# The reciprocal square roots of a hybrid trunk's norms, moved from VectorE to a power operation on GpSimd

## The chip, the cores and the metric

The kernel runs on one core of one Trainium2 chip. The metric is the time of one execution in device microseconds (us), lower is better.

## The reference

One layer of a decoder trunk on 2048 rows of width 1024. The input is normed and projected; four head groups work on the projection; each is normed per head (three of them) and gated, and an output projection with a norm of its own is added to the input:

```python
def _rmsnorm(x, g):
    y = x32 * lax.rsqrt(jnp.mean(x32 * x32, axis=-1, keepdims=True) + EPS)
    return (y * g.astype(F32)).astype(x.dtype)
def _head_rmsnorm(o, g):
    return o * lax.rsqrt(jnp.mean(o * o, axis=-1, keepdims=True) + EPS) * g.astype(F32)
def _l2norm(t):
    return t * lax.rsqrt(jnp.sum(t * t, axis=-1, keepdims=True) + EPS)
...
h = _rmsnorm(x, norm_pre[i])
p = jnp.einsum('bld,dc->blc', h, w_in[i]).astype(F32)
y_ret  = retention(...)        # chunks of 64, then _head_rmsnorm and silu(gate)
y_dn   = gated delta rule(...) # q, k through _l2norm; a recurrence over chunks of 64; _head_rmsnorm, gate
y_s5   = diagonal state space, gelu, a gate
y_gla  = gated linear attention(...)  # chunks of 16, a recurrence; _head_rmsnorm, gate
o = jnp.einsum('bld,md->...', concatenate([y_ret, y_dn, y_s5, y_gla]), w_out[i])
x = x + _rmsnorm(o, norm_post[i])
```

## The kernel before

The 2048 rows are 16 tiles of 128. The program runs in stages, by the trace at these times: to 140 us the input norms (`p0_x`, one call a tile) with the weights' scaling, projections and the first retention tiles; to 330 us the rest of retention (`ret_rest`, a tile a call); 330 to 612 us GLA (`phase_gla`, 16 iterations, two tiles' scores in flight, with S5 work put between); 612 to 1060 us DeltaNet (`phase_dn`, eight steps of two tiles: `dn_pre` makes decays and the norms of q and k, `dn_back` runs the recurrence over the state VS); from 1060 us the output (`phase_out`, whose `back` makes one tile and whose fronts load and transpose later ones, two ahead).

Wherever a norm needs 1/sqrt(v), `rsqrt` (L171) makes it with nine VectorE instructions on a [128, n] tile, n being 1, 4 or 8: a first guess from the bits of v (L175, L176), then two rounds of polynomial steps (L181 to L187), each needing the one before. It is called from four places, 88 calls in all:

- `p0_x`, 16 times (n = 1, tile names x..): ScalarE squares and sums (L484), VectorE scales and adds eps (v, L486), rsqrt, and ScalarE makes h (L491).
- `finish` (L345), 48 times (n = 4, names f..), for retention, GLA and DeltaNet, 16 each: ScalarE squares the branch's output o from PSUM into fsq (L349), VectorE sums it per head (fss, L351), scales and adds eps (fv, L354 or, with DeltaNet's eps per head, L356), rsqrt gives fry, L359 multiplies by half the gate's scale (frr), and four multiplications (L363) make o times frr times gate, which goes to memory.
- `dn_pre`, 8 times (n = 8, names d..): rk = rsqrt(kk), sk = kk rk (L1450), and rk squared (L1451), which scales dD and dkgd, and by them the mask dmb (L1459).
- `back`, 16 times (n = 1, names o..): VectorE squares and sums the output of (ojk, L1721), sums the four parts (ost, L1724), makes e2 and ov (L1726, L1728), rsqrt, and xo = ot times r plus xo (L1733), while GpSimd makes ot = of times the gain (L1722).

Each engine executes its instructions in the order in which the scheduler put them. The scheduler takes the program's streams (generators that yield between pieces) and interleaves them by priority; the instructions of a norm so come to stand between those of other tiles. In DeltaNet the recurrence goes through VectorE's VS = dQ - c (L1669) and ScalarE's copy of the next state; in GLA through gS (L1237, VectorE) and gSbd (L1240, GpSimd). GpSimd also does the masks and products of the scores (gE, L1160 to L1176), the S5 powers (s5c, s5O; L608), DeltaNet's dKG (L1659, L1660), the head of the convolution (raw, L1336) and a part of the weights' scaling (w, L243).

Of the kernel before, what the change touches and what calls it, by code (L numbers as in the profile page):

```python
# [16 lines left out]
EPS = 1e-6  # L17
XS = 6
BLK = 1040
MAGIC = float(0x5F1FFFF9)  # L20
# [125 lines left out]
class Trunk:  # L146
# [24 lines left out]
    def rsqrt(self, pool, v, n, tag, mul=1.0):  # L171

        nc = self.nc
        yi = self.t(pool, [128, n], tag + "y", I32)
        nc.vector.tensor_scalar(yi, v.bitcast(I32), 1, None, op0=ALU.arith_shift_right)  # L175
        nc.vector.tensor_scalar(yi, yi, -1.0, MAGIC, op0=ALU.mult, op1=ALU.add)  # L176
        y = yi.bitcast(F32)
        t = self.t(pool, [128, n], tag + "t")
        V = nc.vector
        m = 0.375 * mul  # L180
        V.tensor_tensor(t, y, y, op=ALU.mult)  # L181
        V.scalar_tensor_tensor(t, t, -0.703952253 * m, v, op0=ALU.mult, op1=ALU.mult)
        V.scalar_tensor_tensor(y, t, 2.38924456 * 0.703952253 * m, y, op0=ALU.add, op1=ALU.mult)
        V.tensor_tensor(t, y, y, op=ALU.mult)
        V.scalar_tensor_tensor(t, t, 1.0 / (m * m), v, op0=ALU.mult, op1=ALU.mult)
        V.scalar_tensor_tensor(t, t, -10.0 / 3.0, t, op0=ALU.add, op1=ALU.mult)
        V.scalar_tensor_tensor(y, t, 5.0, y, op0=ALU.add, op1=ALU.mult)  # L187
        return y
# [183 lines left out]
    def setup(self):  # L372
        nc, A = self.nc, self.A
# [11 lines left out]
        keep = self.keep  # L385
# [3 lines left out]
        self.gains = self.t(keep, [128, 8], "gains")  # L389
        self.su = self.dram.tile([self.NT * 128, 256], F32, name="su_d", tag="su_d")  # L390
# [84 lines left out]
    def p0_x(self, i, quick=False):  # L475

        nc, A, P = self.nc, self.A, self.P0
# [584 lines left out]
    def ret_rest(self, i):  # L1062
# [38 lines left out]
        self.finish(P, po, g, self.half(self.W["rg"][1]), 0, i)  # L1101

    def phase_gla(self, last, then, mid, side):
# [118 lines left out]
        def output(i, S, Sbd):  # L1222
# [18 lines left out]
            self.finish(P, po, g[i], self.half(self.W["gg"][1]), 3, i)  # L1241
# [162 lines left out]
    def dn_pre(self, u, kq, out):  # L1404
# [39 lines left out]
        nc.vector.tensor_scalar(epsq, p4[:, :, 1], 4 * EPS, 256 * EPS, op0=ALU.add, op1=ALU.mult)  # L1444
# [109 lines left out]
    def dn_back(self, u, f, T, state, gates):  # L1554
# [99 lines left out]
        for t in range(2):  # L1654
# [25 lines left out]
            self.finish(P, po.rearrange("p h t -> p (h t)"), gates.pop(i), self.half(self.W["dg"][1]), 1, i, eps=f["epsq"][:, t])  # L1680
# [3 lines left out]
    def phase_out(self):  # L1684
# [6 lines left out]
        nc.sync.dma_start(npost, A["npost"])  # L1691
        size = {"xo": 1024, "yo": 1024, "y16": 2048, "yT": 2048}
# [4 lines left out]
        def back(i, xs, yT, s, steps):  # L1697
# [137 lines left out]
```

## Time and profile before

| what | value |
|---|---|
| median of 3 runs | 1251.0 us (1250.88 to 1252.23) |
| profiled execution | 1254.29 us, span 1252.3 us |
| TensorE (PE) busy | 1123.0 us, 90% |
| VectorE (DVE) busy | 942.7 us, 75%, 3434 instructions |
| ScalarE (ACT) busy | 474.1 us, 38% |
| GpSimd (POOL) busy | 443.0 us, 35%, 826 instructions |
| chain that ended last | DVE 40%, PE 23%, ACT 6%, issue 6%, DMA 2%, POOL 1% |

The span is the time from the first to the last instruction of the profiled execution; that execution's own time holds some 2 us more. Busy times of PE contain the modelled ends of pipelined matmuls, so a busy PE is not one at its peak. The chain is followed back from the last instruction to what released it or to the instruction before it on its engine; "issue" is time in which an engine waited for nothing that shows.

### The profile page before, as it was taken

How to read it: one execution, taken by the hardware profiler on the slowest of the kernel's cores; microseconds unless marked ns; L12 is line 12 of the kernel's file. 1: busy time of each engine (PE TensorE's matmuls, PEld its weight loads, DVE VectorE, ACT ScalarE, POOL GpSimd, SP SyncE). 2: the span in 40 equal slices, each digit the busy share in tenths (PEclk: the TensorE clock that was granted, in tenths of full speed). 3: DMA queues.
4: the chain of work that ended last, by engine and by line, in shares of the span. 5: the costliest groups of instructions: out<-in, count | busy, mean ns of one | idle time of the engine just before them, and what ended most of it. 6: DMA issues, size and time to landing. Idle time of an engine off the chain costs nothing.

```text
span 1252.3 us, 37313 instructions
## 1 busy us (share of the span) xinstructions
PE 1123.0 (90%) x15175; PEld 931.3 (74%) x15175; DVE 942.7 (75%) x3434; ACT 474.1 (38%) x1012; POOL 443.0 (35%) x826
## 2 busy tenths in 40 slices
PE   3989899999898888998688899989989999899997
PEld 2778788888787776777576777766767778788886
DVE  7779655447888889998878787786787645778786
ACT  6633421125343434452334233433433453434332
POOL 3211111112755556563432423623513312334332
PEclk9989999999899999898989899998999999899999
DMA  8766611101211111221312121122113625566653
GB/s 284 154 162 160 139 64 67 32 30 52 62 30 35 28 32 26 68 59 23 86 45 33 27 39 20 27 54 38 27 51 61 171 64 163 155 183 172 190 133 104
DMA packets 186907, 104.90 MB, mean 84 GB/s; under 512 B 158000, under 2 KB 173552, under 8 KB 184560
## 3 DMA queue, kind: packets, MB, share of 16 engines
q1 hardware_dynamic: 186160, 102.00, 31.7%
q8 instruction: 119, 1.95, 0.6%
q10 hardware_dynamic: 576, 0.52, 0.1%
q14 instruction: 52, 0.43, 0.1%
HBM read 59.43 MB, written 26.23 MB: 68 GB/s over the span
## 4 chain that ended last, share of the span: by engine, by line
DVE 40%; PE 23%; ACT 6%; issue 6%; DMA 2%; POOL 1%; DVEq 0%; ACTq 0%; SPq 0%; POOLq 0%
PE pa L282 5%; PE pa L290 5%; DVE cva L1342 3%; DVE w L246 3%; DVE gsT L1216 3%; PE o L1711 2%; DVE gE L1176 2%; DVE ojk L1721 2%; DVE s5r L608 2%; PE c L1674 2%; DVE fsq L363 1%; PE o L1678 1%; ACT gE L1164 1%; PE t L1441 1%; ACT gE L1165 1%
## 5 line engine op out<-in xcount | busy, mean ns | idle before, releaser
L282 PE MATMUL pa<-w,xT 128*128 128x256 f16 x3072 | 384.2, 279 | 9.9 <-DVE w L246 4.0
L282 PEld LDWEIGHTS <-xT 128*128 128x128 f16 x3456 | 336.1, 100 | 73.9 <-issue 16.6
L290 PE MATMUL pa<-xT,w 128*128 128x256 f16 x1536 | 210.9, 285 | 24.5 <-ACT raw L1337 13.7
L290 PEld LDWEIGHTS <-w 128*128 128x128 f16 x1536 | 148.3, 102 | 56.3 <-issue 30.4
L1711 PE MATMUL o<-w,yT 128*128 128x256 f16 x1344 | 154.8, 275 | 7.4 <-DMA yT<-y 7.4
L1711 PEld LDWEIGHTS <-yT 128*128 128x128 f16 x1344 | 132.0, 99 | 27.6 <-DMA yT<-y 10.1
L1722 POOL TENSOR_TENSOR ot<-of,npost 128x256 f32<-128x256 f32 x64 | 59.4, 946 | 62.1 <-ACT of L1720 62.0
L1342 DVE SCALAR_TENSOR_TENSOR cva<-raw,cw,cva 128x256 f32<-128x256 f32 x144 | 78.8, 551 | 1.3
L1336 POOL COPY raw<-raw 128x3 f32<-128x3 f32 x48 | 14.6, 310 | 120.4 <-DVE cva L1342 71.4
L349 ACT ACTIVATE fsq<-o 128x256 f32<-128x256 f32 x48 | 18.3, 380 | 93.5 <-PE o L1100 58.2
L1176 POOL TENSOR_TENSOR gE<-gE,gk 128x64 f32<-128x64 f32 x112 | 33.2, 329 | 57.3 <-ACT gE L1165 48.9
L246 DVE SCALAR_TENSOR_TENSOR w<-stg,wgs,w 128x256 f16<-128x256 f32 x96 | 48.7, 542 | 5.9 <-POOL w L243 5.7
L282 PE MATMUL pa<-wsu,xT 128*128 128x280 f16 x384 | 49.8, 287 | 3.3 <-ACT wsu L245 1.9
L1053 POOL TENSOR_TENSOR ropq<-ropm,ropn 128x256 f32<-128x256 f32 x16 | 12.6, 790 | 107.0 <-DVE ropn L1050 79.5
L1312 ACT ACTIVATE cvt<-cva 128x256 f32<-128x256 f32 x48 | 19.8, 413 | 80.9 <-DVE cva L1342 59.7
L1721 DVE SCALAR_TENSOR_TENSOR ojk<-of 128x256 f32<-128x256 f32 x64 | 40.6, 635 | 11.1 <-ACT of L1720 8.0
L321 ACT ACTIVATE th<-pa,hd 128x256 f32<-128x256 f32 x64 | 30.0, 468 | 45.7 <-PE pa L282 45.3
L351 DVE TENSOR_REDUCE fss<-fsq 128x4 f32<-128x256 f32 x48 | 19.9, 414 | 32.8 <-ACT fsq L349 32.6
L1189 PE MATMUL sc<-gE 32*32 32x32 f32 (+1 forms) x2944 | 42.5, 203 | 1.4 <-ACT gsT L1219 1.4
L1189 PEld LDWEIGHTS sc<-gE 32*32 32x32 f32 (+1 forms) x2944 | 34.9, 107 | 10.7 <-issue 2.9
L1216 DVE TENSOR_TENSOR gsT<-gs,gs 32x64 f32<-32x64 f32 x128 | 40.6, 317 | 2.2
L1084 POOL TENSOR_TENSOR sg<-sbd,cst 64x128 f32<-64x128 f32 x30 | 12.8, 425 | 82.3 <-DVE sbd L1085 72.9
(430 smaller groups left out, 2282.2 us busy)
## 6 DMA issues: line engine op xcount, KB each, us to landing
x<-in_x SPq DMA_DIRECT2D x16, 512.0 KB, 4.5
stg<-in_wi SPq DMA_DIRECT2D x8, 1024.0 KB, 4.7
yo<-y_d SPq DMA_DIRECT2D x14, 512.0 KB, 4.5
xo<-in_x SPq DMA_DIRECT2D x14, 512.0 KB, 3.6
out<-xo SPq DMA_DIRECT2D x13, 512.0 KB, 3.7
y_d<-fsq SPq DMA_DIRECT2D x48, 128.0 KB, 1.9
xT<-in_wi SPq DMA_DIRECT2D x4, 1024.0 KB, 6.9
rope<-in_rope SPq DMA_DIRECT2D x16, 256.0 KB, 2.8
```

The source lines that it names most:

```text
L246: nc.vector.scalar_tensor_tensor(dst[:, 1, k, :], st[:, k, :], gs[:, k:k + 1], dst[:, 0, k, :], op0=ALU.mult, op1=ALU.subtract)
L282: yield lambda k=k, i=i, a=a, b=b: self.nc.tensor.matmul(out, xt[:, a, k, t0:t0 + 128], w[:, b, k, :], start=(k == 0 and i == 0), stop=(k ...
L290: yield lambda k=k, i=i, a=a, b=b: self.nc.tensor.matmul(out, w[:, b, k, c0:c0 + 128], xt[:, a, k, :], start=(k == 0 and i == 0), stop=(k ...
L321: nc.scalar.activation(th, ps[0], AF.Tanh, scale=self.half(dsc))
L608: (eng or self.nc.vector).tensor_tensor(out, a, b, op=op)
L1176: eng.tensor_tensor(x, x, src.rearrange("p (n w) -> p n w", w=2 * b)[:, :, a:a + b], op=ALU.mult)
L1189: nc.tensor.matmul(box[0][po:po + pn, e, c0:c0 + rh.shape[1]], lh[r], rh[r], start=True, stop=True, tile_position=(32 * (2 * hp + e), col))
L1216: nc.vector.tensor_tensor(sv[cb, :, cb], s2[cb], s1[cb, :, 2, :], op=ALU.add)
L1342: nc.vector.scalar_tensor_tensor(a, raw[:, j, k:k + 256], cw[:, 4 * j + k:4 * j + k + 1], a, op0=ALU.mult, op1=ALU.add)
L1711: nc.tensor.matmul(o, yT[:, a, k, :], w[:, b, k, :], start=(k == 0 and q == 0 and j % per == 0), stop=(k == 7 and q == 2 and j % per == pe ...
L1721: nc.vector.scalar_tensor_tensor(jk, of[:, cs], 1.0, of[:, cs], op0=ALU.mult, op1=ALU.mult, accum_out=so[:, j:j + 1])
L1722: nc.gpsimd.tensor_tensor(t1[:, cs], of[:, cs], npost[:, cs], op=ALU.mult)
```

## The change

`rsqrt` now consists of an optional addition of eps and one tensor_tensor with `pow` on GpSimd, against a table `expo` that holds -0.5 and 0.5. The scalings by 1/64, 1/1024 and 2^6 are folded into constants that multiply elsewhere (`half` with 4.0, the square's scale, the gain `npost` times 32), so that fv, v and ov are gone; `frr` and `oe` go to GpSimd. In `dn_pre` rk squared becomes a VectorE reciprocal of kk, and sk a power of 0.5 on GpSimd. Cut to its core:

```diff
-    def rsqrt(self, pool, v, n, tag, mul=1.0):
...
+    def rsqrt(self, pool, v, e, n, tag):
+        g = self.nc.gpsimd
+        y = self.t(pool, [128, n], tag)
+        if e is not None:
+            g.tensor_scalar(y, v, e, None, op0=ALU.add)
+            v = y
+        g.tensor_tensor(y, v, self.expo[:, 0, 0:n], op=ALU.pow)
         return y
...
     def finish(self, pool, o, g, h4, branch, tile_i, eps=None):
...
-        v = self.t(pool, [128, 4], "fv")
-        if eps is None:
-            nc.vector.tensor_scalar(v, ss, 1.0 / 64, EPS, op0=ALU.mult, op1=ALU.add)
-        else:
-            nc.vector.scalar_tensor_tensor(v, ss, 1.0 / 64, eps, op0=ALU.mult, op1=ALU.add)
-        r = self.rsqrt(pool, v, 4, "fr")
+        if eps is not None:
+            nc.gpsimd.tensor_tensor(ss, ss, eps, op=ALU.add)
+        r = self.rsqrt(pool, ss, 64 * EPS if eps is None else None, 4, "fr")
         rr = self.t(pool, [128, 4], "frr")
-        nc.vector.tensor_scalar(rr, r, hd, None, op0=ALU.mult)
+        nc.gpsimd.tensor_scalar(rr, r, h4, None, op0=ALU.mult)
...
+        self.expo = self.t(keep, [128, 2, 8], "expo")
+        nc.gpsimd.memset(self.expo[:, 0], -0.5)
+        nc.gpsimd.memset(self.expo[:, 1], 0.5)
...
-        nc.vector.tensor_scalar(v, ss, 1.0 / 1024, EPS, op0=ALU.mult, op1=ALU.add)
-        r = self.rsqrt(P, v, 1, "xr", mul=2.0 ** XS)
+        q = 32.0 * 2.0 ** XS
+        nc.scalar.activation(h16[:, 0, :].bitcast(BF16), xs, AF.Square, scale=1.0 / q, accum_out=ss)
+        r = self.rsqrt(P, ss, 1024 * EPS / q ** 2, 1, "xr")
...
-        rk = self.rsqrt(P, kk, 8, "dr")
         sk = self.t(P, [128, 8], "dsk")
-        nc.vector.tensor_tensor(sk, kk, rk, op=ALU.mult)
-        nc.vector.tensor_tensor(rk, rk, rk, op=ALU.mult)
+        nc.gpsimd.tensor_tensor(sk, kk, self.expo[:, 1], op=ALU.pow)
+        rk = self.t(P, [128, 8], "dr")
+        nc.vector.reciprocal(rk, kk)
...
+        nc.gpsimd.tensor_scalar(npost, npost, 32.0, None, op0=ALU.mult)
...
-            nc.vector.tensor_scalar(e2, s, s, EPS, op0=ALU.mult, op1=ALU.mult)
-            v = self.t(P, [128, 1], "ov")
-            nc.vector.scalar_tensor_tensor(v, st, 1.0 / 1024, e2, op0=ALU.mult, op1=ALU.add)
-            r = self.rsqrt(P, v, 1, "or")
+            nc.gpsimd.tensor_scalar(e2, s, s, 1024 * EPS, op0=ALU.mult, op1=ALU.mult)
+            r = self.rsqrt(P, st, e2, 1, "or")
```

The order on each engine changes with it. Three places follow. Line numbers of the changed kernel are about nine lower (L1669 is L1660 there, L363 is L351, L977 is L968).

VectorE, GLA, the finish that the trace of before has at 473 us; before:

```order
L351 TENSOR_REDUCE fss_6883<-fsq_6881 128x4 [waits Activation_49]
L354 TENSOR_SCALAR fv_6885<-fss_6883 128x4 [waits DVE_49]
L1237 SCALAR_TENSOR_TENSOR gS_6877<-gS_6540,gel_5986,pa_6872 128x64 [waits PE_49]
L175 TENSOR_SCALAR fry_6887<-fv_6885 128x4 [waits DVE_49]
...
L1207 TENSOR_TENSOR gpm_6961<-sc_1131_6906,glamask_4524 128x384 [waits PE_49]
...
L359 TENSOR_SCALAR frr_6898<-fry_6887,hd_829_4902 128x4 [waits DVE_49]
L1212 TENSOR_TENSOR gs_1134_6965<-gs_1133_6963 128x64
L363 SCALAR_TENSOR_TENSOR fsq_6900<-o_6862,frr_6898,ggg_6651 128x64 [waits DMAHW1_49,DVE_49]
```

The same place after, on VectorE, and then on GpSimd:

```order
L341 TENSOR_REDUCE fss_6520<-fsq_6518 128x4 [waits Activation_49]
L1228 SCALAR_TENSOR_TENSOR gS_6514<-gS_6187,gel_5643,pa_6509 128x64 [waits PE_49]
L351 SCALAR_TENSOR_TENSOR fsq_6527<-o_6499,frr_6525,ggg_6288 128x64 [waits DMAHW0_49,DVE_49,Pool_49]
L351 SCALAR_TENSOR_TENSOR fsq_6527<-o_6499,frr_6525,ggg_6288 128x64 x3
L1147 SCALAR_TENSOR_TENSOR gE_6660<-cst_75,ggk_6658 128x128 [waits DMAHW1_49,PE_49]
L1198 TENSOR_TENSOR gpm_6588<-sc_1060_6533,glamask_4209 128x384 [waits PE_49]
```

```order
L1170 TENSOR_TENSOR gkl_6330<-gE_6317,gk_5939 128x128 [waits PE_49]
L175 TENSOR_SCALAR fr_6522<-fss_6520 128x4 [waits DVE_49]
L177 TENSOR_TENSOR fr_6522<-fr_6522,expo_79 128x4 [waits Pool_49]
L347 TENSOR_SCALAR frr_6525<-fr_6522,hd_813_4813 128x4 [waits Pool_49]
L1160 COPY gel_6331<-gE_6317 128x1 [waits DVE_49]
L1231 TENSOR_TENSOR gSbd_6516<-gS_6514,cst_75 128x256
```

The steps of the next scores (gE, gpm, gs), which stood between the instructions of the norm, now stand behind fsq.

VectorE, DeltaNet, the first finish of a step (745 us in the trace of before), where VS is the recurrence; before:

```order
L351 TENSOR_REDUCE fss_12876<-fsq_12874 128x4 [waits Activation_49]
L356 SCALAR_TENSOR_TENSOR fv_12878<-fss_12876,depsq_11582 128x4 [waits DVE_49]
L175 TENSOR_SCALAR fry_12880<-fv_12878 128x4 [waits DVE_49]
...
L323 SCALAR_TENSOR_TENSOR dgg_12915<-th_12913,pa_12840 128x256 [waits Activation_49]
L186 SCALAR_TENSOR_TENSOR frt_12883<-frt_12883 128x4 [waits DVE_49]
L1669 TENSOR_TENSOR VS_12793<-dQ_12758,c_12917 64x256 [waits PE_49]
...
L363 SCALAR_TENSOR_TENSOR fsq_12893<-o_12792,frr_12891,dgg_12545 128x64 [waits DMAHW1_49,DVE_49]
```

After, on VectorE, and then on GpSimd:

```order
L341 TENSOR_REDUCE fss_12325<-fsq_12323 128x4 [waits Activation_49]
L351 SCALAR_TENSOR_TENSOR fsq_12332<-o_12241,frr_12330,dgg_11994 128x64 [waits DVE_49,DMAHW1_49,PE_49,Pool_49]
L351 SCALAR_TENSOR_TENSOR fsq_12332<-o_12241,frr_12330,dgg_11994 128x64 x3
L313 SCALAR_TENSOR_TENSOR dgg_12354<-th_12352,pa_12289 128x256 [waits Activation_49]
L1660 TENSOR_TENSOR VS_12242<-dQ_12207,c_12356 64x256 [waits PE_49]
```

```order
L1650 TENSOR_TENSOR dKG_12338<-dkh_11379,dkgd_11081 64x256 [waits PE_49]
L1651 TENSOR_TENSOR dKG_12338<-cst_75,dgl_11083 64x256
L1650 TENSOR_TENSOR dKG_12338<-dkh_11379,dkgd_11081 64x256
L1651 TENSOR_TENSOR dKG_12338<-cst_75,dgl_11083 64x256
L344 TENSOR_TENSOR fss_12325<-fss_12325,depsq_11071 128x4 [waits DVE_49,Pool_49]
L177 TENSOR_TENSOR fr_12328<-fss_12325,expo_79 128x4 [waits Pool_49]
L347 TENSOR_SCALAR frr_12330<-fr_12328,hd_1681_10914 128x4 [waits Pool_49]
```

VS has moved from ahead of fsq to behind it.

VectorE, output, the tenth tile (1143 us in the trace of before); y belongs to a later tile; before:

```order
L1724 TENSOR_REDUCE ost_18554<-so_18413 128x1 [waits DVE_49]
L1728 SCALAR_TENSOR_TENSOR ov_18558<-ost_18554,oe_2713_18556 128x1 [waits DVE_49]
L175 TENSOR_SCALAR ory_18560<-ov_18558 128x1 [waits DVE_49]
L1726 TENSOR_SCALAR oe_2761_18898<-ysc_18504 128x1
L977 SCALAR_TENSOR_TENSOR y_2705_18502<-yo_18231,ysc_18504,y_2705_18502 128x1024 [waits DMAHW6_49,Activation_49]
L176 TENSOR_SCALAR ory_18560<-ory_18560 128x1 [waits DVE_49]
...
L1733 SCALAR_TENSOR_TENSOR xo_18171<-ot_2710_18540,ory_18560,xo_18171 128x1024 [waits DMAHW3_49,DMAHW4_49,DVE_49,Pool_49]
```

After:

```order
L1716 TENSOR_REDUCE ost_17754<-so_17613 128x1 [waits DVE_49]
L1724 SCALAR_TENSOR_TENSOR xo_17391<-ot_2563_17740,or_17758,xo_17391 128x1024 [waits DMAHW3_49,DMAHW1_49,Pool_49]
L968 SCALAR_TENSOR_TENSOR y_2558_17702<-yo_17441,ysc_17704,y_2558_17702 128x1024 [waits DMAHW7_49,Activation_49]
L1713 SCALAR_TENSOR_TENSOR ojk_17902,so_17774<-of_17900 128x256 [waits DVE_49,Activation_49] x2
```

xo and y have changed places.

## Rows read from the trace of the kernel before

**Rows 1.** The page, part 1: busy us, share of the span, instructions.

```profile
PE 1123.0 (90%) x15175; PEld 931.3 (74%) x15175; DVE 942.7 (75%) x3434; ACT 474.1 (38%) x1012; POOL 443.0 (35%) x826
```

**Rows 2.** The page, part 4: the chain that ended last, by engine.

```profile
DVE 40%; PE 23%; ACT 6%; issue 6%; DMA 2%; POOL 1%; DVEq 0%; ACTq 0%; SPq 0%; POOLq 0%
```

**Rows 3.** Windows by stage: from:to, length, busy us (instructions), clock, DMA share, GB/s.

```profile
0.00:140.00 140.00, 108.01 (x907) 89.22 (x908) 112.22 (x603) 70.18 (x118) 29.99 (x51) 0.95 0.75 192
140.00:330.00 190.00, 187.31 (x1830) 163.41 (x1829) 102.76 (x367) 51.34 (x91) 40.29 (x86) 1.00 0.16 50
330.00:612.00 282.00, 245.94 (x5127) 204.39 (x5125) 251.71 (x867) 113.06 (x273) 151.43 (x363) 0.95 0.18 40
...
660.00:1060.00 400.00, 366.79 (x5488) 288.87 (x5486) 287.34 (x1023) 150.60 (x347) 132.33 (x220) 0.96 0.25 56
1060.00:1252.00 192.00, 177.04 (x1527) 154.17 (x1525) 147.67 (x469) 73.05 (x155) 67.17 (x74) 0.97 0.57 162
```

**Rows 4.** The chain that ended last, output: start us, us, what.

```profile
1233.74 10.67 PE o L1711 x96
```

**Rows 5.** Groups by line, VectorE: shapes, count, busy us, mean ns, idle before.

```profile
L175 DVE TENSOR_SCALAR fry<-fv 128x4 int32<-128x4 int32 x48 | 13.2, 274 | 0.7
...
L186 DVE SCALAR_TENSOR_TENSOR frt<-frt 128x4 f32<-128x4 f32 x48 | 8.7, 180 | 0.8
```

**Rows 6.** Groups by line, GpSimd.

```profile
L1176 POOL TENSOR_TENSOR gE<-gE,gk 128x64 f32<-128x64 f32 x112 | 33.2, 329 | 57.3 <-ACT gE L1165 48.9 <-ACT gk L1136 8.4
...
L1169 POOL COPY gel<-gE 128x1 f32<-128x1 f32 x16 | 3.1, 197 | 5.8 <-ACT gE L1165 4.1 <-DVE gS L1237 1.7
```

**Rows 7.** The chain that ended last, GLA, one finish.

```profile
473.42 0.17 DVE fv L354
473.60 0.18 DVE gS L1237
...
477.35 0.36 DVE frr L359
...
477.84 0.77 DVE fsq L363 x4
```

**Rows 8.** Timeline of GpSimd, same finish: start, us, line, operation, [idle before].

```profile
472.45 1.48 POOL L608 TENSOR_TENSOR s5c<-pd,bb 128x128 f32<-128x128 f32 x4
473.89 0.45 POOL L1179 TENSOR_TENSOR gkl<-gE,gk 128x128 f32<-128x128 f32 x1
```

**Rows 9.** Timeline of VectorE, same finish.

```profile
475.77 0.55 DVE L1207 TENSOR_TENSOR gpm<-sc,glamask 128x384 f32<-128x384 f32 x1
```

**Rows 10.** Timeline of VectorE, DeltaNet, the first finish of a step.

```profile
745.19 0.42 DVE L351 TENSOR_REDUCE fss<-fsq 128x4 f32<-128x256 f32 x1 [2.04 <-ACT fsq L349]
...
747.94 0.42 DVE L323 SCALAR_TENSOR_TENSOR dgg<-th,pa 128x256 f32<-128x256 f32 x1
...
748.35 0.41 DVE L1669 TENSOR_TENSOR VS<-dQ,c 64x256 f32<-64x256 f32 x1
...
749.54 0.85 DVE L363 SCALAR_TENSOR_TENSOR fsq<-o,frr,dgg 128x64 f32<-128x64 f32 x4
```

**Rows 11.** Timeline of GpSimd, same finish.

```profile
746.27 0.62 POOL L1660 TENSOR_TENSOR dKG<-cst,dgl 64x256 f32<-64x256 f32 x1
```

**Rows 12.** The chain that ended last, DeltaNet, one dn_pre.

```profile
759.31 0.34 DVE dry L175
...
765.36 0.15 DVE dmb L1459
```

**Rows 13.** Groups by line, ScalarE.

```profile
L491 ACT ACTIVATE h<-x,xry 128x1024 f16<-128x1024 f32 x14 | 16.1, 1147 | 26.4 <-DVE xry L187 21.4 <-DVE cm L608 2.2 <-DVE wv L234 2.1
```

**Rows 14.** Timeline of VectorE, output, the tenth tile.

```profile
1144.07 1.28 DVE L977 SCALAR_TENSOR_TENSOR y<-yo,ysc,y 128x1024 f16<-128x1024 f32 x1
...
1147.70 1.28 DVE L1733 SCALAR_TENSOR_TENSOR xo<-ot,ory,xo 128x1024 f32<-128x1024 f32 x1
```

**Rows 15.** Timeline of GpSimd, same tile.

```profile
1144.41 2.20 POOL L1722 TENSOR_TENSOR ot<-of,npost 128x256 f32<-128x256 f32 x2 [0.58 <-ACT of L1720]
```

More of the change, by code (lines that the diff above doesn't have):

```diff
@@ L19 @@
 BLK = 1040
-MAGIC = float(0x5F1FFFF9)
 SEGS = ["su", "rq", "rk", "rv", "rg", "gqk", "gv", "gg", "dq", "dk", "dv", "dg", "sg"]
@@ L168, in psA @@
         return self.t(self.pA, [128, 512], "pa")
-    def rsqrt(self, pool, v, n, tag, mul=1.0):
[L173 to L187, printed above, removed]
+    def rsqrt(self, pool, v, e, n, tag):
[5 more added lines that the diff above has]
+        g.tensor_tensor(y, v, self.expo[:, 0, 0:n], op=ALU.pow)
         return y
@@ L335, in gate, with half, finish @@
         return g[0]
-    def half(self, dsc):
-        key = id(dsc)
+    def half(self, dsc, f=0.5):
+        key = id(dsc), f
         if key not in self._half:
             h = self.t(self.keep, [128, 1], self.uid("hd"))
-            self.nc.vector.tensor_scalar(h, dsc, 0.5, None, op0=ALU.mult)
+            self.nc.vector.tensor_scalar(h, dsc, f, None, op0=ALU.mult)
             self._half[key] = (h, dsc)
         return self._half[key][0]
-    def finish(self, pool, o, g, hd, branch, tile_i, eps=None):
+    def finish(self, pool, o, g, h4, branch, tile_i, eps=None):
         nc = self.nc
@@ L483, in p0_x @@
         h16 = self.t(P, [128, 2, 1024], "h16", F16)
-        nc.scalar.activation(h16[:, 0, :].bitcast(BF16), xs, AF.Square, accum_out=ss)
-        v = self.t(P, [128, 1], "v")
-        nc.vector.tensor_scalar(v, ss, 1.0 / 1024, EPS, op0=ALU.mult, op1=ALU.add)
-        r = self.rsqrt(P, v, 1, "xr", mul=2.0 ** XS)
+        q = 32.0 * 2.0 ** XS
+        nc.scalar.activation(h16[:, 0, :].bitcast(BF16), xs, AF.Square, scale=1.0 / q, accum_out=ss)
+        r = self.rsqrt(P, ss, 1024 * EPS / q ** 2, 1, "xr")
         if quick:
@@ L1100, in ret_rest @@
             nc.tensor.matmul(po[:, h * 64:(h + 1) * 64], sT[:, h // 2, h % 2, :], v[:, h, :], start=False, stop=(h == 3))
-        self.finish(P, po, g, self.half(self.W["rg"][1]), 0, i)
+        self.finish(P, po, g, self.half(self.W["rg"][1], 4.0), 0, i)
     def phase_gla(self, last, then, mid, side):
@@ L1240, in output @@
                 nc.gpsimd.tensor_tensor(Sbd, S.unsqueeze(1).to_broadcast([128, 4, 64]), blk.unsqueeze(2).to_broadcast([128, 4, 64]), op=ALU.mult)
-            self.finish(P, po, g[i], self.half(self.W["gg"][1]), 3, i)
+            self.finish(P, po, g[i], self.half(self.W["gg"][1], 4.0), 3, i)
             return S, Sbd
@@ L1443, in dn_pre @@
         epsq = self.t(P, [128, 2, 4], "depsq", bufs=3)
-        nc.vector.tensor_scalar(epsq, p4[:, :, 1], 4 * EPS, 256 * EPS, op0=ALU.add, op1=ALU.mult)
+        nc.vector.tensor_scalar(epsq, p4[:, :, 1], 4 * EPS, 16384 * EPS, op0=ALU.add, op1=ALU.mult)
         kk = self.t(P, [128, 8], "dkk")
@@ L1679, in dn_back @@
             yield
-            self.finish(P, po.rearrange("p h t -> p (h t)"), gates.pop(i), self.half(self.W["dg"][1]), 1, i, eps=f["epsq"][:, t])
+            self.finish(P, po.rearrange("p h t -> p (h t)"), gates.pop(i), self.half(self.W["dg"][1], 4.0), 1, i, eps=f["epsq"][:, t])
             VS = VSn
```

## The prediction
> **What bounds the kernel now.** I read the page's busy line first, then the chain of waits, then the stages, and only then single norms. The busy line [rows 1] shows TensorE at 1123.0 of 1252.3 us and VectorE at 942.7, with GpSimd far below at 443.0. Taken alone it would say that a change on VectorE is worth nothing. The chain that ended last [rows 2] says otherwise: 40% of it is VectorE and 23% TensorE, so VectorE's order decides for long stretches.
>
> The table by stage [rows 3] tells where. From 140 to 330 us (retention and projections) TensorE is busy for 187.31 of 190 us and VectorE for 102.76: nothing that VectorE saves there can show. From 330 to 612 (GLA) VectorE is busy for 251.71 of 282 us, 89%, and GpSimd for 151.43. From 660 to 1060 (DeltaNet) TensorE has 366.79 of 400 and VectorE 287.34; neither is full, and the work goes back and forth through the recurrence. From 1060 on (output) TensorE has 177.04 of 192. A tile's 96 matmuls take 10.67 us [rows 4], 111 ns each, out of 192 / 16 = 12.0 us a tile. Up to 140 us VectorE is busy for 112.22 and TensorE for 108.01 of 140, while the transfers take 0.75 of the DMA engines.
>
> **The change, part by part.** Gone are 88 calls x 9 = 792 instructions of the rsqrt, and with them the scalings around it (48 fv, 48 frr, 16 v, 32 in the output, 8 net in dn_pre): 944 on VectorE, some 200 us of its 942.7. One instruction on 128x4 takes between 180 and 274 ns on average [rows 5]; the eleven of one finish come to 118 us over 48 finishes, 2.46 each. About 235 come to GpSimd: an addition of eps, the power, and in finish a multiplication by the half gain.
>
> The price of the new ones. The small addition and multiplication are nearest to the GpSimd copy of 128x1, 197 ns [rows 6]; I take 0.2 us. The power is in no row. From below it is bounded by the same 0.2 us. From above I take 2 us, seven times the 128x64 tensor_tensor of 329 ns [rows 6], since a power needs many steps per element where those need one, and 512 elements are few. I choose 0.6 us, about twice the row that it is nearest to as a tensor_tensor (329 ns). A finish then takes GpSimd 0.2 + 0.6 + 0.2 = 1.0 us.
>
> The rule that speaks against this is in the Trainium skill's GPSIMD Engine Reference, section Engine selection: two-input elementwise work belongs on VectorE, GpSimd being about two times slower. The 197 ns copy against VectorE's 180 [rows 5, 6] shows no factor of two at this size; by the page the addition and the multiplication would take 0.36 us each, 0.32 us more per finish, and at the 36 us lost per us of price worked out below the gain would be 25 - 12 = 13 us.
>
> *GLA, 16 finishes: 19 us gained.* In the finish of 473 us the eleven removed lines hold 2.67 us of the chain between the start of fv at 473.42 and fsq at 477.84 (eleven pieces, first fv, last frr) [rows 7]. The other 1.75 us there are gaps and steps of the next scores, put between them. In the changed order the multiplication fsq stands one instruction (gS or gpm) behind the reduction, and so VectorE, which goes in order, stands still until GpSimd is through. What fills GpSimd then: the s5c until 473.93, then gkl until 474.34 (gkl starts at 473.89) [rows 8]; the three new ones come behind gkl and end at about 475.35. VectorE is through with gS at 473.8 [rows 7] and waits 1.6 us. In every other iteration GpSimd is free: 1.0 us, less the 0.55 us of gpm [rows 9], which stands between there, is a wait of 0.45. The mean is 1.05, so an iteration gains 2.67 - 1.05 = 1.6 us. I take off 0.4 for what is now queued behind the power on GpSimd: gel and gSbd, which the next output product needs, and the gE products. 1.2 x 16 = 19. Bounds: 0.45 to 2.2 an iteration at the same price of the power, 7 to 35 us.
>
> *DeltaNet, 16 finishes and 8 dn_pre: 2 us gained.* The first finish of a step stands ahead of the recurrence. Its reduction ends at 745.61, and VS, on which the next state's matmuls wait, is issued at 748.35, before the old chain has ended [rows 10]. In the changed order VS stands behind fsq. GpSimd has four dKG products first, until 746.27 + 0.62 = 746.9 [rows 11]; then 1.0 us, to 747.9; the four fsq take 0.85 and the gate dgg 0.42 [rows 10], so VS starts at 749.2, 0.85 us later. That is 8 x 0.85 = 7 us lost, on the recurrence. The second finish of a step loses 2.46 us of VectorE work for a wait of about 1.0, and its multiplication is partly mixed with convolution work that would have run anyway: 0.6 x 8 = 5 won. In dn_pre the chain runs through the removed lines from dry at 759.31 to dmb at 765.36, mixed with convolutions of the same length [rows 12]; ten instructions of about 0.18 us go, 1.8 us, of which I count a quarter as TensorE has other work: 0.5 x 8 = 4. Sum +2, bounds -15 (both finishes wait behind GpSimd) to +20 (VS is not late, as TensorE is).
>
> *Start, 16 norms: 3 us gained.* ScalarE waited 21.4 us for xry before it made h [rows 13]; ten instructions (v and the nine) become two, at most 1.8 us against 0.8, and VectorE is relieved of some 32 us out of 112. But the new pair queues among the weight scalings on GpSimd, and the transfers at 0.75 [rows 3] don't get faster. Bounds -4 and +10. *140 to 330: 0*, hidden by TensorE; if that cover went, 16 finishes x 1.4 us = 22 would be there.
>
> *Output, 16 tiles: 1 us gained.* Now the next tile's y (1144.07) goes ahead of most of the old chain, and xo follows at 1147.70 [rows 14]. In the changed order xo waits for GpSimd directly behind the reduction ost, and y stands behind xo. GpSimd's own last two ot products end at 1144.41 + 2.20 = 1146.6 [rows 15], then 0.8 us: xo at 1147.4 and y only at 1148.7, 4.6 us late. TensorE sets the pace (10.67 of 12.0 us are matmuls), so I expect this to be hidden by the two tiles that are in flight. What is left is the tail, where ten instructions of under 0.2 us become 0.8: about +1. Bounds -4 (the last y late) and +5.
>
> Sum: 19 + 2 + 3 + 0 + 1 = 25 us. The profiled execution took 1254.29 (span 1252.3 and 2.0 around it), so it would take 1229.3. The median of the three runs, 1251.0, lies 3.3 lower, and the forecast with it: **1226 us**.
>
> **The rivals.** (a) *The power is dear, and VectorE stands still for it: slower.* Each us of price beyond 0.6 costs 16 us in GLA, 12 in DeltaNet (where all of the first and half of the second finishes hold VectorE), 4 at the start and 4 in the output: 36. The gain of 25 is gone at 0.6 + 25 / 36 = 1.3 us. At 2 us it is 1226 + 1.4 x 36 = 1276. For it: no row shows a power. Against it: the small GpSimd rows lie at 0.2 to 0.35 us [rows 6]. (b) *GpSimd's queue eats the gain: no change.* GpSimd is busy for 54% of GLA [rows 3], every wait is like the first kind (1.6) and the knock-on twice as large, so GLA gives 0.3 x 16 = 5, and DeltaNet loses 7: about 1250. The page cited above would make this likelier. (c) *The waits are covered: far faster.* If the power is at 0.2 and the waits fall where VectorE had been waiting for others, GLA gives 2.67 x 16 = 43, the start 10, DeltaNet 10 and the output 4: 67, or 1184. For it: VectorE's 40% of the chain. That the work does not go is excluded: the changed order holds none of these instructions.
>
> **How the numbers follow.** Forecast (a gain of 8 to 45 us) 0.48; (a) 0.27; (b) 0.07; (c) 0.18. A measurement of this kernel can tell about 0.2%, 2.5 us, from no change. Faster by more: 0.48 + 0.18 = 0.66. Same: 0.07. Slower: 0.27. The range takes in the forecast's bounds, most of (c) and half of (a), up to a power of 1.7 us: 1188 to 1265, which leaves 0.05 below and 0.14 above. The likeliest case alone holds 1206 to 1243.
>
> **What would show it.** VectorE near 740 us busy and GpSimd near 530. Right: L177 on GpSimd at 0.4 to 0.9 us; an idle time of VectorE ahead of fsq, released by GpSimd's frr, of some 1 us in GLA; GLA iterations about 1.2 us shorter than now (282 / 16 = 17.6); DeltaNet's steps unchanged; the output's pace unchanged, with y later. Wrong: a power of over 1.3 us, VectorE's idle time ahead of fsq above 2.5 us in GLA, TensorE waiting for yT in the output, or a DeltaNet step that has grown by more than 2 us.

## The result, and the profile after

The changed kernel takes 1326.62 us (median of 4 runs, 1326.18 to 1327.78) against 1251.62 for the kernel before: the ratio is 1.0596, interval 1.0576 to 1.0615. It is 6% slower, and outside the predicted range. The profiled execution's span is 1324.4 us. The page, part 1, against [rows 1]:

```profile
PE 1154.1 (87%) x15175; PEld 950.3 (72%) x15175; DVE 797.8 (60%) x2493; ACT 476.0 (36%) x1012; POOL 557.0 (42%) x1061
```

VectorE has lost 145 us of work and GpSimd has got 114. The prediction had put VectorE near 740 us. The instructions taken off it make up the 200 us that it counted, but others took longer (ojk 753 ns in place of 635), and 797.8 us are left. The largest of all waits is new. Here is its line in the list of waits (us in total, times, longest), then GpSimd's new instructions by form (count | busy us, mean ns | idle us before), and then the three groups of fsq:

```profile
DVE fsq L351 <- POOL frr L347: 125.5, 48, 5.4
```

```profile
L177 POOL TENSOR_TENSOR fr<-fr,expo 128x4 f32<-128x4 f32 x32 | 33.2, 1038 | 2.7
...
L177 POOL TENSOR_TENSOR fr<-fss,expo 128x4 f32<-128x4 f32 x16 | 16.4, 1023 | 1.1
...
L1440 POOL TENSOR_TENSOR dsk<-dkk,expo 128x8 f32<-128x8 f32 x8 | 15.2, 1903 | 4.3 <-DVE dkk L1438 4.2
...
L347 POOL TENSOR_SCALAR frr<-fr,hd 128x4 f32<-128x4 f32 x48 | 14.7, 307 | 4.6
...
L177 POOL TENSOR_TENSOR xr<-xr,expo 128x1 f32<-128x1 f32 x16 | 9.4, 586 | 1.3
...
L175 POOL TENSOR_SCALAR fr<-fss 128x4 f32<-128x4 f32 x32 | 8.4, 261 | 39.3 <-DVE fss L341 35.2 <-DVE scc L596 2.3
```

```profile
L351 DVE SCALAR_TENSOR_TENSOR fsq<-o,frr,dgg 128x64 f32<-128x64 f32 x64 | 14.0, 277 | 50.6 <-POOL frr L347 50.6
L351 DVE SCALAR_TENSOR_TENSOR fsq<-o,frr,rgg 128x64 f32<-128x64 f32 x64 | 13.8, 278 | 29.3 <-POOL frr L347 29.3
L351 DVE SCALAR_TENSOR_TENSOR fsq<-o,frr,ggg 128x64 f32<-128x64 f32 x64 | 13.8, 278 | 45.6 <-POOL frr L347 45.6
```

VectorE waits in front of fsq in every one of the 48 finishes, 2.6 us on average: 50.6 us in DeltaNet, 29.3 in retention, 45.6 in GLA. Three of these waits follow, from the timelines. In GLA, VectorE and then GpSimd:

```profile
487.02 0.41 DVE L341 TENSOR_REDUCE fss<-fsq 128x4 f32<-128x256 f32 x1
487.35 0.54 DVE L1198 TENSOR_TENSOR gpm<-sc,glamask 128x384 f32<-128x384 f32 x1
491.52 0.86 DVE L351 SCALAR_TENSOR_TENSOR fsq<-o,frr,ggg 128x64 f32<-128x64 f32 x4 [3.62 <-POOL frr L347]
```

```profile
485.86 1.64 POOL L599 TENSOR_TENSOR s5T<-s5c,s5c 128x256 f32<-128x256 f32 x2 [0.76 <-DVE s5r L599]
487.45 0.40 POOL L599 TENSOR_TENSOR s5c<-pw,s5bc 128x128 f32<-128x128 f32 x1
...
489.02 0.62 POOL L1231 TENSOR_TENSOR gSbd<-gS,cst 128x256 f32<-128x256 f32 x1
489.73 0.23 POOL L175 TENSOR_SCALAR fr<-fss 128x4 f32<-128x4 f32 x1
490.04 1.04 POOL L177 TENSOR_TENSOR fr<-fr,expo 128x4 f32<-128x4 f32 x1
491.18 0.31 POOL L347 TENSOR_SCALAR frr<-fr,hd 128x4 f32<-128x4 f32 x1
```

The sum fss is there at 487.4; GpSimd is among its S5 products and begins with the root only at 489.7, 2.3 us late; the three instructions then take 1.76 us. The same happens in DeltaNet's first finish of a step, where VS, the recurrence, now stands behind fsq (against [rows 10]):

```profile
786.14 0.42 DVE L341 TENSOR_REDUCE fss<-fsq 128x4 f32<-128x256 f32 x1 [2.04 <-ACT fsq L339]
790.00 0.86 DVE L351 SCALAR_TENSOR_TENSOR fsq<-o,frr,dgg 128x64 f32<-128x64 f32 x4 [3.45 <-POOL frr L347]
790.78 0.41 DVE L313 SCALAR_TENSOR_TENSOR dgg<-th,pa 128x256 f32<-128x256 f32 x1
791.11 0.41 DVE L1660 TENSOR_TENSOR VS<-dQ,c 64x256 f32<-64x256 f32 x1
```

From the start of fss to VS it is 4.97 us here and was 748.35 - 745.19 = 3.16 before. In the second finish of a step (fss ends at 751.48) GpSimd has more ahead of it, the power of dsk, the products dST and four dKG; GpSimd and then VectorE:

```profile
749.09 1.67 POOL L1440 TENSOR_TENSOR dsk<-dkk,expo 128x8 f32<-128x8 f32 x1 [3.42 <-DVE dkk L1438]
...
751.34 1.97 POOL L1493 TENSOR_TENSOR dST<-ckq,dE 64x128 f32<-64x128 f32 x4
...
755.77 0.19 POOL L344 TENSOR_TENSOR fss<-fss,depsq 128x4 f32<-128x4 f32 x1
```

```profile
757.49 0.86 DVE L351 SCALAR_TENSOR_TENSOR fsq<-o,frr,dgg 128x64 f32<-128x64 f32 x4 [5.41 <-POOL frr L347]
```

To see where the time went, the span is cut at the starts of the reductions in each trace: the 16th of finish (end of retention), the 17th to the 32nd (GLA), the 33rd to the 48th (DeltaNet), the first of the output to the end. "Between" is the rest. Each row is one execution; some rows belong to kernels of the next section.

| profiled span, us | to 16th | GLA | DeltaNet | output | between | sum |
|---|---|---|---|---|---|---|
| before | 319.9 | 247.8 | 347.4 | 189.9 | 147.3 | 1252.3 |
| changed | 331.4 | 272.7 | 379.5 | 190.9 | 149.9 | 1324.4 |
| finish on VectorE | 323.8 | 249.3 | 345.8 | 185.4 | 145.9 | 1250.2 |
| only finish changed | 328.0 | 272.3 | 364.2 | 188.6 | 157.8 | 1310.9 |
| power replaced by product | 328.4 | 258.0 | 363.3 | 190.3 | 151.6 | 1291.6 |
| fsq later | 327.9 | 257.0 | 368.4 | 189.3 | 149.7 | 1292.3 |
| no root in finish | 323.7 | 235.8 | 327.8 | 188.5 | 150.3 | 1226.1 |
| root not awaited | 324.9 | 236.3 | 331.0 | 190.0 | 151.0 | 1233.2 |
| gate first | 324.4 | 242.2 | 336.4 | 188.6 | 149.3 | 1240.9 |

Of the 72 us that the span grew, DeltaNet has 32.1, GLA 24.9, the start with retention 11.5, the stretches between 2.6 and the output 1.0.

TensorE does the same matmuls but is busy for longer. The windows of the GLA and the DeltaNet column, before and after (as in [rows 3]):

```profile
357.20:605.00 247.80, 218.76 (x4620) 182.44 (x4620) 221.22 (x782) 96.65 (x233) 131.76 (x325) 0.95 0.17 38
696.50:1043.90 347.40, 321.34 (x4805) 251.51 (x4804) 249.51 (x892) 129.58 (x298) 117.48 (x194) 0.96 0.24 53
```

```profile
372.90:645.60 272.70, 231.57 (x4590) 188.49 (x4590) 193.06 (x610) 96.39 (x232) 150.00 (x363) 0.90 0.15 34
735.40:1114.90 379.50, 331.55 (x4795) 258.40 (x4795) 210.74 (x665) 130.97 (x300) 148.63 (x246) 0.91 0.21 49
```

The mean granted clock fell from 0.95 to 0.90 in GLA and from 0.96 to 0.91 in DeltaNet, and TensorE's busy time grew by 12.8 and 10.2 us, though it stood still for more of the windows (busy for 85% and 87% of them, where it was 88% and 92%). A part of the loss may so come by the clock; no run separates it.

### The profile page after: what moved, and what is told of

Its sections match the earlier page's. It is cut to its first block, busy times and chain, and to the rows that moved or that the text cites. A ratio compares the mean times of both kernels' runs of the same rounds, so it can differ in the third digit from the quotient of the medians.

```text
span 1324.4 us, 36605 instructions
## 1 busy us (share of the span) xinstructions
PE 1154.1 (87%) x15175; PEld 950.3 (72%) x15175; DVE 797.8 (60%) x2493; ACT 476.0 (36%) x1012; POOL 557.0 (42%) x1061
## 5 line engine op out<-in xcount | busy, mean ns | idle before, releaser
L272 PE MATMUL pa<-w,xT 128*128 128x256 f16 x3072 | 390.8, 283 | 17.5 <-DVE ropn L1041 5.4
L272 PEld LDWEIGHTS <-xT 128*128 128x128 f16 x3456 | 341.3, 102 | 86.7 <-issue 20.2
L280 PE MATMUL pa<-xT,w 128*128 128x256 f16 x1536 | 221.0, 294 | 31.3 <-DVE dgg L313 13.5
L280 PEld LDWEIGHTS <-w 128*128 128x128 f16 x1536 | 152.9, 105 | 68.8 <-issue 36.4
L1333 DVE SCALAR_TENSOR_TENSOR cva<-raw,cw,cva 128x256 f32<-128x256 f32 x144 | 73.4, 511 | 2.0
L1713 DVE SCALAR_TENSOR_TENSOR ojk<-of 128x256 f32<-128x256 f32 x64 | 48.2, 753 | 18.4 <-ACT of L1712 15.4
L1327 POOL COPY raw<-raw 128x3 f32<-128x3 f32 x48 | 15.7, 333 | 98.2 <-DVE cva L1333 73.7
L236 DVE SCALAR_TENSOR_TENSOR w<-stg,wgs,w 128x256 f16<-128x256 f32 x96 | 44.7, 518 | 8.6 <-POOL w L233 8.3
L351 DVE SCALAR_TENSOR_TENSOR fsq<-o,frr,dgg 128x64 f32<-128x64 f32 x64 | 14.0, 277 | 50.6 <-POOL frr L347 50.6
L1650 POOL TENSOR_TENSOR dKG<-dkh,dkgd 64x256 f32<-64x256 f32 x32 | 19.7, 616 | 57.8 <-PE c L1665 57.7
```

The costliest lines, as they stand in the source:

```text
L236: nc.vector.scalar_tensor_tensor(dst[:, 1, k, :], st[:, k, :], gs[:, k:k + 1], dst[:, 0, k, :], op0=ALU.mult, op1=ALU.subtract)
L272: yield lambda k=k, i=i, a=a, b=b: self.nc.tensor.matmul(out, xt[:, a, k, t0:t0 + 128], w[:, b, k, :], start=(k == 0 and i == 0), stop=(k ...
L280: yield lambda k=k, i=i, a=a, b=b: self.nc.tensor.matmul(out, w[:, b, k, c0:c0 + 128], xt[:, a, k, :], start=(k == 0 and i == 0), stop=(k ...
L1333: nc.vector.scalar_tensor_tensor(a, raw[:, j, k:k + 256], cw[:, 4 * j + k:4 * j + k + 1], a, op0=ALU.mult, op1=ALU.add)
L1713: nc.vector.scalar_tensor_tensor(jk, of[:, cs], 1.0, of[:, cs], op0=ALU.mult, op1=ALU.mult, accum_out=so[:, j:j + 1])
```

## The experiments

The theory after the result (W) is that VectorE's standing still ahead of fsq is the loss. Its rivals are the power's own price wherever it is used (P), the input norms (N), and the room that the new instructions take in GpSimd's queue (Q).

**Which of the four places.** One kernel has finish as before, the other has nothing but finish changed:

```diff
-        r = self.rsqrt(pool, ss, 64 * EPS if eps is None else None, 4, "fr")
...
+        r = self.rsqrt9(pool, v, 4, "fr")
```

That is the line of the first; rsqrt9 is the nine steps, and fv, frr and the constants are as before too.

> The changed kernel with finish as before: its nine-step reciprocal root, fv and frr on VectorE for all 48 head norms; the input norms, the norms of q and k and the output norm stay on GpSimd's power. Theory W (VectorE stands still ahead of fsq until GpSimd's three instructions and whatever is queued before them are through; that wait, 125.5 us over 48 finishes, is the loss): 1240 to 1255 us, GLA and DeltaNet as long as before. Rival N (the 16 us that are lost before GLA come from the input norms' place in GpSimd's queue): about 1265, with the first GLA finish still near 373 us. Rival P (the power's own price, wherever it is used): between, about 1265 to 1280.

> The opposite half: finish with GpSimd's power as changed, the three other places with the nine-step root on VectorE as before. W: 1315 to 1330 us, all of the loss. N: about 1308, 16 us less of it. P: about 1300, as 40 of the 88 powers are gone.

Finish on VectorE: 1253.45 us, ratio 1.0017 (0.9991 to 1.0043), no difference. Only finish changed: 1313.58 us, 1.0489 (1.0459 to 1.0519). The first is in W's range and below both rivals' figures. The second is just below W's range and above the rivals'. So finish makes most of the loss, 61 of 75 us. Two smaller things show in the table. The input norms on GpSimd cost 3.9 us before the end of retention (323.8 against 319.9), a quarter of what N said. And DeltaNet is 15 us shorter with only finish changed than with all (364.2 against 379.5), though 8 us of it come back in the stretches between. VectorE's wait there is 36.0 us in place of 50.6:

```profile
L372 DVE SCALAR_TENSOR_TENSOR fsq<-o,frr,dgg 128x64 f32<-128x64 f32 x64 | 14.2, 277 | 36.0 <-POOL frr L368 36.0
```

With finish on VectorE the new dn_pre costs nothing. The reading that fits is that its 1.9 us power of 128x8 adds to the queue in which VectorE waits, and is harmless where VectorE doesn't; no run changes that power alone.

**The price of the power.** A product in the same place, with the same table:

```diff
-        r = self.rsqrt(pool, ss, 64 * EPS if eps is None else None, 4, "fr")
+        r = self.rsqrt(pool, ss, 64 * EPS if eps is None else None, 4, "fr", ALU.mult)
```

> The changed kernel with the power in finish replaced by a product with the same table, so that the head norms' factor is another number: the instruction's shape, place and waits stay, only its duration falls, from 1.04 to some 0.25 us. P (the price of the power is the cause): back to 1250 or below. W (the wait is the queue and three instructions in a row as much as the power): VectorE's wait falls by 0.8 us a finish, the time by 0.8 x 32 to 48, to 1288 to 1300 us.

1292.47 us, 1.0313 (1.0287 to 1.0339), as W expected. The instruction fell from 1038 to 200 ns:

```profile
L177 POOL TENSOR_TENSOR fr<-fr,expo 128x4 f32<-128x4 f32 x32 | 6.4, 200 | 2.7
```

0.84 us less in each finish brought 1326.6 - 1292.5 = 34 us, 41 us per us. With a power at the price of a product the kernel would still be 3% slower.

**The order.** fsq is traced later and tied in issue order behind another VectorE instruction, in GLA behind the gs of the next scores, in DeltaNet's first finish of a step behind VS (there the second finish's fsq also goes one piece later, and the PSUM tile of the output is taken behind VS):

```diff
-            self.finish(P, po, g[i], self.half(self.W["gg"][1], 4.0), 3, i)
+            return S, Sbd, self.finish(P, po, g[i], self.half(self.W["gg"][1], 4.0), 3, i, later=True)
...
+                with self.tc.issue_after(self.mark):
+                    second()
```

> The changed kernel with the multiplication fsq put later in VectorE's order: in GLA behind the next scores' gpm and gs, in DeltaNet's first finish of a step behind VS, which continues the recurrence. Power, price and GpSimd's order stay. W: the wait ahead of fsq falls from 45.6 to below 15 us in GLA and to about half of 50 in DeltaNet; the two stages together get 35 to 50 us shorter, 1275 to 1292 us. P: no change, 1320 or more, as the power costs what it did.

1298.2 us, 1.0357 (1.0326 to 1.0388), between W's range and P's. GLA got 15.7 us shorter and DeltaNet 11.1; 28 us in all. The wait of VectorE fell only from 125.5 to 99.0 us, in GLA from 45.6 to 25.2 and in DeltaNet from 50.6 to 44.7:

```profile
DVE fsq L352 <- POOL frr L347: 99.0, 44, 7.0
```

```profile
L352 DVE SCALAR_TENSOR_TENSOR fsq<-o,frr,ggg 128x64 f32<-128x64 f32 x64 | 15.1, 279 | 25.4 <-POOL frr L347 25.2
L352 DVE SCALAR_TENSOR_TENSOR fsq<-o,frr,dgg 128x64 f32<-128x64 f32 x64 | 14.1, 277 | 44.7 <-POOL frr L347 44.7
```

The order matters, but W's numbers were too good. In GLA the two or three instructions put ahead of fsq do not cover GpSimd's 1.8 us and the queue before it. In DeltaNet the edit did its work in the first finish of a step and the wait moved to the second. One step, VectorE and then what GpSimd had ahead of the second root:

```profile
767.03 0.86 DVE L352 SCALAR_TENSOR_TENSOR fsq<-o,frr,dgg 128x64 f32<-128x64 f32 x4 [0.82 <-POOL frr L347]
...
785.49 0.86 DVE L352 SCALAR_TENSOR_TENSOR fsq<-o,frr,dgg 128x64 f32<-128x64 f32 x4 [5.10 <-POOL frr L347]
```

```profile
777.13 3.57 POOL L1499 TENSOR_TENSOR dST<-ckq,dE 64x128 f32<-64x128 f32 x4
...
782.02 1.66 POOL L1446 TENSOR_TENSOR dsk<-dkk,expo 128x8 f32<-128x8 f32 x1
```

From the second step on the first finish waits 1.0 us or less, where it was 2.5 to 3.9; the second finish waits 5.1 to 7.0 us in five of the eight steps. To put the waiting instruction later helped only where GpSimd's queue was short by then.

**What the relief is worth, and what the wait costs.** One kernel leaves out the root of the head norms in finish; the other computes it on GpSimd and does not use it. Both multiply by the gate's scale instead, in this line:

```diff
-            nc.vector.scalar_tensor_tensor(y[:, s], o[:, s], rr[:, h:h + 1], g[:, s], op0=ALU.mult, op1=ALU.mult)
+            nc.vector.scalar_tensor_tensor(y[:, s], o[:, s], h4, g[:, s], op0=ALU.mult, op1=ALU.mult)
```

> The changed kernel with nothing between the reduction and fsq in finish: no power, no addition, no product with the half gain, and fsq takes the gate's scale instead of the norm's factor, so the head norms are left out. It shows what VectorE's relief alone is worth, without any wait. If the prediction's price of the removed instructions holds (2.67 us an iteration in GLA, and what it counted in DeltaNet), 1185 to 1205 us. If they mostly filled time in which VectorE would have waited for others (theory C, cover), 1225 to 1245 us.

> The changed kernel with GpSimd's three instructions of finish in place, at their full price, but fsq takes the gate's scale and does not wait for them (their result is left unused, the head norms' factor is left out). If VectorE's standing still is the loss (W): within 10 us of the run without them. If it is GpSimd's own queue, in which gSbd, gel, gE and dKG stand behind the power (theory Q): 30 us or more above that run, towards 1300.

No root: 1229.84 us, 0.9836 (0.9814 to 0.9858). Not awaited: 1235.39 us, 0.9871 (0.9846 to 0.9896). The first is as the cover theory C expected, the second as W did. This cuts the result into three. Taking 118 us of small instructions [rows 5] off VectorE, with no wait in their place, gives 21 us (1250.5 - 1229.8, the other three places' changes included). GpSimd's room costs some 5.5 us, little more than the spread of each kernel's runs. Anything that the three instructions cost VectorE's own by running beside them is in these 5.5 us too. Awaiting the result costs 1326.6 - 1235.4 = 91 us. That is W, and it speaks against Q. What the clock may cost is within the 91 us: with the root not awaited, the windows of GLA and DeltaNet have a granted clock of 0.94 and 0.97, and TensorE is busy there for 532.3 us, against 563.1 in the changed kernel.

**The change in dn_pre and the output alone**, with finish and the input norms as before:

> The change in dn_pre and the output alone: finish and the input norms on VectorE as before, the reciprocal and the power for q and k, the power for the output norm. From the stages of the run with finish on VectorE, where the output was 3.7 us shorter, DeltaNet 1.6 us shorter and the start 3.9 us longer: 1244 to 1249 us, 0.3 to 0.6% below the kernel before. If the output's gain came only from the start's other phase, no difference.

1247.57 us, 0.9976 (0.996 to 0.9992): a small gain, as expected. The output, 189.9 us before, takes 185.1. That is not the new code's alone: the same output code takes 185.1 to 190.9 us in the ten traces that have it.

**A form that does not wait.** VectorE multiplies o by the gate and its scale at once, and GpSimd, which has the root, does the last product:

```diff
+        og = self.t(pool, [128, 4, 64], "fog", bufs=1)
+        nc.vector.scalar_tensor_tensor(og.rearrange("p h d -> p (h d)"), o, h4, g, op0=ALU.mult, op1=ALU.mult)
         r = self.rsqrt(pool, ss, 64 * EPS if eps is None else None, 4, "fr")
-        rr = self.t(pool, [128, 4], "frr")
-        nc.gpsimd.tensor_scalar(rr, r, h4, None, op0=ALU.mult)
...
+        nc.gpsimd.tensor_tensor(y, og, r.unsqueeze(2).to_broadcast([128, 4, 64]), op=ALU.mult)
```

> The changed kernel with finish in another form and the same result: VectorE multiplies o by the gate and its scale right behind the reduction (one instruction of 128x256, which waits for nothing on GpSimd), and GpSimd multiplies that product by the norm's factor behind its power, one 128x256 instruction of about 0.95 us in place of the product with the half gain. If VectorE's wait for GpSimd is the whole loss of the change: near the run that does not await the power (1235), with some us for the longer time on GpSimd and less for the 0.4 us that VectorE saves in each finish: 1230 to 1245 us. If the power on GpSimd costs in another way (its queue, contention), 1270 or more.

> The same, with the input norms back on VectorE's nine steps. In the pair of runs with finish on VectorE the input norms on GpSimd cost 3.5 us before the end of retention; if that adds, 3 to 5 us less than the run with the gate first. If the start's loss hangs on finish's waits in the first four retention tiles instead, no difference.

> The run with the gate first, but the root of finish made by VectorE's nine steps again (all else as in that run): VectorE multiplies o by gate and scale, makes the root, GpSimd multiplies the two. If the gain over the kernel before comes from taking the root off VectorE (with nothing waiting for it): near the kernel before, 1248 to 1256 us. If it comes from the product with the gate, which frees the PSUM tile at once and is one instruction in place of four: as fast as the run with the gate first, 1240 to 1246.

Gate first: 1243.58 us, 0.9926 (0.99 to 0.9952), 0.7% faster than the kernel before. In GLA, VectorE and then GpSimd:

```profile
463.93 0.41 DVE L341 TENSOR_REDUCE fss<-fsq 128x4 f32<-128x256 f32 x1
464.26 0.48 DVE L346 SCALAR_TENSOR_TENSOR fog<-o,hd,ggg 128x256 f32<-128x256 f32 x1
464.65 0.55 DVE L1196 TENSOR_TENSOR gpm<-sc,glamask 128x384 f32<-128x384 f32 x1
465.12 0.62 DVE L1145 TENSOR_TENSOR_SCAN gE<-cst,ggk 128x128 f32<-128x128 f32 x1
```

```profile
467.61 0.23 POOL L175 TENSOR_SCALAR fr<-fss 128x4 f32<-128x4 f32 x1
467.92 1.07 POOL L177 TENSOR_TENSOR fr<-fr,expo 128x4 f32<-128x4 f32 x1
469.07 0.61 POOL L349 TENSOR_TENSOR fsq<-fog,fr 128x256 f32<-128x256 f32 x1
```

GpSimd's root begins 3.3 us behind the sum, later than in the changed kernel, and VectorE goes on with the next scores. With the input norms back on VectorE: 1243.28 us, 0.9926, no difference, so the 3.5 us that they cost with finish on VectorE did not add. With the nine steps in finish and the gate first: 1254.13 us, 1.0024 (1.0006 to 1.0042). So the new product alone gives nothing; the gain is the root's move to GpSimd, once VectorE does not wait for it.

## Why the prediction was wrong

*By stage.* The forecast was a gain of 19 us in GLA, 2 in DeltaNet, 3 at the start and 1 in the output. Measured was a loss of 24.9, 32.1, 11.5 and 1.0. Two of the prediction's own signs of being wrong are there: VectorE's idle time ahead of fsq above 2.5 us in GLA, and a DeltaNet step longer by more than 2 us (32.1 us over the seven and a half steps of the column).

*The bound, and GLA: the step that failed.* "An iteration gains 2.67 - 1.05 = 1.6 us" was wrong in both terms. The 2.67 us that the removed lines held on the chain of one finish [rows 7] were taken as a gain. Without any wait GLA became 247.8 - 235.8 = 12 us shorter, 0.8 us for each of the 15 iterations that the column spans; most of the room went to something else, which no run singles out. The wait was priced at 1.05 and came to 45.6 / 16 = 2.85 us. Most of that error is in the text "in every other iteration GpSimd is free". There it is not, since s5T, s5c, gel and gSbd stand ahead (3.62 us above). These eight finishes wait 29.7 us, where 8 x 0.45 = 3.6 were forecast; the other eight wait 15.9, where 8 x 1.6 = 12.8 were. The changed order of GpSimd holds those rows, and so does the trace of before, in the finish whose sum starts at 459.39, the one ahead of the finish that the prediction read:

```profile
458.75 1.79 POOL L608 TENSOR_TENSOR s5T<-s5c,s5c 128x256 f32<-128x256 f32 x2 [3.26 <-DVE s5r L608]
460.51 0.59 POOL L608 TENSOR_TENSOR s5c<-pw,s5bc 128x128 f32<-128x128 f32 x1
461.06 1.06 POOL L608 TENSOR_TENSOR s5c<-pw,ncim 128x128 f32<-128x128 f32 x2
462.09 0.45 POOL L608 TENSOR_TENSOR s5c<-pw,s5bc 128x128 f32<-128x128 f32 x1
```

The place from which the sum was taken was of the other kind, with gkl ahead. The 0.4 us taken off for what is queued behind the power was too much: the whole stage has 236.3 us with the root on GpSimd but not awaited, against 235.8 without it.

*DeltaNet.* The mechanism was right for the first finish of a step: VS stands behind fsq, behind four dKG products. The price was not: VS was put 0.85 us late and is 4.97 - 3.16 = 1.8 us late in the finish shown. The second finish was put at a wait of 1.0 us and a gain, and waits 3.1 us on average (24.5 us over eight). Together they wait 50.6 us; awaiting costs 379.5 - 331.0 = 48.5 us there. The queue holds more than dKG (masks, dST, the dsk power). The relief, 347.4 - 327.8 = 19.6 us, is what the optimistic bound gave.

*The price of the power.* 0.6 us was chosen, 1.04 was measured; the upper bound of 2 us was six times its row of 329 ns, not seven. The slope that the prediction gave the finishes was 28 us per us (16 in GLA and 12 in DeltaNet, the other 8 of its 36 being the start and the output); 41 was found. At 41 the power explains 0.44 x 41 = 18 of the 101 us between forecast and result, and all three instructions of finish (0.23, 1.04 and 0.31, 1.76 us with their gaps, against 1.0) some 30. The run with the product is the test: there a finish takes GpSimd 1.76 - 0.84 = 0.92 us, about what was priced, and the kernel is at 1292 and not at 1226. The other two thirds lie in the queue and in the relief that was taken too high.

*The rivals.* (a) named the mechanism, VectorE standing still, and its side, but made the power's price decide, with a turning point at 1.3 us. There is none in what was measured: at 1.04 us the kernel is 6% and at 0.2 us 3% slower. (b) named the queue, but took every wait in GLA at 1.6 us, where they are 2.85 on average and up to 4.7, and so expected no change. (c) is excluded as far as its size goes: even with no wait GLA gives 12 us and not 43.

*The rule that spoke against the change* was on the right side, but not for its reason. The Trainium skill's GPSIMD Engine Reference, Engine selection, gives about two times slower for operations with two inputs and calls those with one input roughly line-rate. In retention and GLA the addition of eps is that of a constant, and the product with the half gain takes one number per row; both have one input tensor, so the prediction's 0.36 us apiece took the wrong half of that row. At 128x4 the addition took 0.261 and the product 0.307 us on GpSimd, against 0.241 for the same product on VectorE before: a factor of 1.3, not two. DeltaNet's addition, with two inputs, took 0.19 (at 755.77 above). A product with two inputs, gE of 128x64, takes 329 ns on GpSimd [rows 6] and as much on VectorE:

```profile
L1176 DVE TENSOR_TENSOR gE<-gE,gq 128x64 f32<-128x64 f32 x112 | 28.8, 324 | 7.2 <-ACT gE L1165 7.0
```

What made the change slow was not this rate.

*Start: wrong sign.* 11.5 us were lost. Awaiting finish makes 331.4 - 324.9 = 6.5 of them. The other 5.0 stay undivided: the input norms cost 3.9 with finish on VectorE, but putting them back brought nothing with the gate first. ScalarE's wait for the norm [rows 13] fell from 21.4 to 12.0 us (now for GpSimd's xr), and the start got no shorter by it. The claim that retention hides all holds from the fourth tile on: from the fourth reduction to the 16th it is 187.4 us before and 188.4 after. *Output: inside its bounds, with the sign wrong.* It took 1.0 us longer where 1 less was forecast. VectorE waits there for GpSimd's power too, 17.6 us ahead of xo, and this wait and y's later place cost no more than that 1.0. What a wait cost went by what stood behind it.

## What to carry to other kernels

Before work is moved from a busy engine to an idle one, look at what that engine has queued at each point where the result is wanted, in every kind of iteration, and at what stands behind the waiting instruction; the share of busy time tells neither. Then let the busy engine need nothing back: here the same move lost 6% with the result awaited and won 0.7% when the last product went along with it. What instructions hold on a chain of waits is not what their removal gives: here 0.8 of 2.67 us came back in a GLA iteration, and 21 us for 118 us of work in all.

## What the runs showed of the hardware

The time of a power on GpSimd grows with the columns: 0.59 us for 128x1, 1.04 for 128x4 and 1.90 for 128x8 (this one with the exponent 0.5, the others with -0.5), about 0.2 us a column, where a product of 128x4 takes 0.20 in all. A product of 128x256 on GpSimd took 0.64 us on average in the kernel with the gate first, where one operand is 128x4 read 64 times over, and 0.95 in the output (ot), where both are 128x256. Left open: the first GLA finish comes 3 to 5 us later after the last one of retention in all kernels whose finish has no nine steps on VectorE (40.6 us without any root against 37.3 before); what it waits for was not tried. Left open too is what the lower clock alone costs.
